# A gated hybrid decoder layer on one core: the first rows of x in one transfer, the gates' weights and a small load later, the gates' products in the second tile

## Chip, cores, metric

One NeuronCore of a Trainium2 chip. The metric is the device time of one execution in microseconds. TensorE is called PE, VectorE DVE, ScalarE ACT, GpSimd POOL, and SyncE, which only issues DMAs here, SP.

## What is computed

The layer has 512 rows of `x` with 2048 columns and multiplies them by one wide matrix; the columns of the result feed two kinds of attention, gates and a merge. Cut to what matters here:

```
h = x @ w_in                                  # (512 x 2048) @ (2048 x 11808)
log_f = log_sigmoid(h[fox_f] + b_f)           # 8 columns
gates = sigmoid(h[nsa_gate])                  # 24 columns
y_a = (fox_attention(..., log_f) * silu(h[fox_z])) @ w_a
y_b = (nsa_attention(..., gates, rel_bias) * silu(h[nsa_z])) @ w_b
out = layer_norm(ALPHA * x + (sigmoid(h[ga]) * y_a + sigmoid(h[gb]) * y_b) @ w_o)
```

The 8 + 24 columns of `log_f` and `gates` are called the gates' columns below.

## The kernel before

All products keep nearly full precision: each operand is split into a high part (`hi`, written by ACT) and a low part (`lo`, written by DVE; helper `split`, lines 96 and 97), and one product of float numbers becomes three matmuls (`mm3`, line 105). The gates' columns have a narrower form with two matmuls (`mm_two`, line 111).

A **tile** of the projection is 128 columns of `h`, computed as `h` transposed: 128 x 512 in one PSUM bank, summed over 16 blocks `k` of 128 rows of `w_in`, 48 matmuls. Its weights come in two **chunks** of 512 KB (tile `wr`, three buffers), each split in two **units** of four blocks `k`. `stream` walks through all units in order; ahead of unit n it splits the weights up to unit n + 3. After every second block `k` the helper `tick` takes one step of each background job in the list `active`, so what a job issues stands in each engine's queue between the matmuls. Each engine works through its own queue in order.

The first tile (columns `C_FZ`) is special, since `x` isn't on the chip yet. `load_x` loads `x`, in pieces of 128 rows by 256 or 512 columns; `transpose_x` transposes four 128 x 128 blocks on PE for each `k` (line 1462), splits the result into `big` (the resident transposed `x`), and lets ACT write one more copy (line 1466). `by_the_way` puts these steps ahead of the blocks k = 2, 4, 8 and 12 of the first tile, and with them the gates' products `gate_cols`: 8 matmuls ahead of k = 8 (with the split of the gates' weights `fgr` into `fgw`), 16 ahead of k = 12, 8 behind the tile. SP's queue, in order: `x` blocks 0 and 1 (four transfers), half of chunk 0, `x` 2 and 3, the other half, `x` 4 to 7, the gates' weights `fgr` (two transfers, 32 and 96 bytes a piece), chunk 1, `x` 8 to 15, chunk 2.

POOL issues small loads ahead of everything: the table `rel_bias` into `rb` and the bias `b_f` into `bf` (line 620), which reads the same 32 bytes for each of 128 partitions and four row blocks. Behind the first tile two jobs start: `lefts` (it waits ten ticks and then subtracts parts of `x` on DVE, line 1071, for later products) and `tables` (bias tables; products on PE at lines 637 and 644). The gates' job in `evac_fg` starts at the same point: transposes at line 681, then some 20 small operations on DVE with a step on ACT twice, then transposes at line 719 of what line 713 wrote, and a scan.

The buffers of tag `om` (16) hold `fgr`, the pieces of `x` and the jobs' small tiles; tag `a` (9) holds eight copies of `x` and the tile `zo` in which a finished tile leaves.

Of the kernel before, what the change touches and what calls it, by code (L numbers as in the profile page):

```python
# [12 lines left out]
F32 = mybir.dt.float32  # L13
# [7 lines left out]
P = 128  # L21
S = 512
D = 2048
KT = D // P
NT = S // P
H = 8
G = 2
HPG = 4
DH = 128
IN_COLS = 11808  # L30
C_FQ, C_FK, C_FV, C_FF, C_FZ = 0, 1024, 2048, 3072, 3080
C_NQ, C_KC, C_VC, C_KS, C_VS, C_KW, C_VW = 4104, 5128, 5384, 5640, 5896, 6152, 6408
C_NG, C_NZ, C_GA, C_GB = 6664, 6688, 7712, 9760
CMP_LEN, CMP_STRIDE, CMP_HID = 32, 16, 256
NCMP = (S - CMP_LEN) // CMP_STRIDE + 1
CP = 32
# [27 lines left out]
def layer(ctx, tc, x, w_in, b_f, pos_k, pos_v, wk1, wk2, wv1, wv2, w_a, w_b, w_o, ln_g, ln_b, rel, onehot, out):  # L64
    nc = tc.nc

    def dram(t, off, ap):
        return bass.AP(tensor=t.tensor, offset=t.offset + off, ap=ap)
# [21 lines left out]
    def bank(tag, bufs):  # L90
        return ps.tile([P, S], F32, name=tag, tag=tag, bufs=bufs)

    def split(hi, lo, src, scale=None):

        if scale is None:
            nc.scalar.activation(hi, src, AF.Copy)  # L96
            nc.vector.tensor_tensor(lo, src, hi.bitcast(F32), op=ALU.subtract)  # L97
        else:
            nc.scalar.activation(hi, src, AF.Copy, scale=scale)
            nc.vector.scalar_tensor_tensor(lo, src, scale, hi.bitcast(F32), op0=ALU.mult, op1=ALU.subtract)  # L100
# [140 lines left out]
    def proj(col, evac, **kw):  # L241
        dense(w_in, IN_COLS, col, D, x_src, evac, **kw)
# [12 lines left out]
    def pool(name):  # L255
        return stage[name][1]
# [42 lines left out]
    def evac_z_out(h):  # L299

        def f(p):
            t = out_tile()[:, 0]
            nc.scalar.activation(t, p, AF.Tanh, scale=0.5)
            nc.vector.scalar_tensor_tensor(t, t, 1.0, p, op0=ALU.add, op1=ALU.mult)
            nc.sync.dma_start(zd[h], t)
        return f
# [295 lines left out]
    def small(name, p, n):  # L602

        return pool("hd").tile([P, S], F32, name=name, tag="om", bufs=KT)[:p, :n]
# [11 lines left out]
    vd = dp.tile([S, H * DH], F32, name="v_d")  # L616
    sigd = [dp.tile([S, D], F32, name=f"sig_d{g}") for g in range(2)]

    nc.gpsimd.dma_start(rb, rel)
    nc.gpsimd.dma_start(bf, dram(b_f, 0, [[0, P], [0, NT], [1, H]]))  # L620

    def tables():
        po = small("po", 2 * CMP_LEN, DH)
        nc.gpsimd.dma_start(po[:CMP_LEN], pos_k[0])
        nc.gpsimd.dma_start(po[CMP_LEN:], pos_v[0])
        neg = small("neg", H, S)
        nc.vector.memset(neg, NEG)
        nc.gpsimd.dma_start(rel_d[:, S:2 * S], neg)
        nc.gpsimd.dma_start(rel_d[:, 2 * S:RL + S - 1], neg[:, :RL - S - 1])
        ohs = [small("oh", BUCKETS, S) for _ in range(2)]  # L630
        for c, oh in enumerate(ohs):
            nc.gpsimd.dma_start(oh, onehot[:, c * S:(c + 1) * S])
        for _ in range(4):
            yield
        for oh, at in zip(ohs, (0, RL + S - 1)):
            m = bank("m", 1)
            nc.tensor.matmul(m[:H], rb, oh, start=True, stop=True)
            tb = small("tb", H, S)
            nc.scalar.activation(tb, m[:H], AF.Copy)
            nc.gpsimd.dma_start(rel_d[:, at:at + S], tb)  # L640
            yield
        copies.append(spread())
        m = bank("m", 1)
        nc.tensor.transpose(m[:, :2 * CMP_LEN], po, ident[:2 * CMP_LEN, :2 * CMP_LEN])
        nc.vector.tensor_copy(posT, m[:, :2 * CMP_LEN])
        yield
# [24 lines left out]
    def evac_fg(p):  # L671

        fg = small("fg", 2 * CP, S)
        nc.vector.tensor_copy(fg, p[:2 * CP])

        def job():
            yield
            yield
            m = bank("m", 1)
            for i in range(NT):  # L680
                nc.tensor.transpose(m[:, i * 2 * CP:(i + 1) * 2 * CP], fg[:, i * P:(i + 1) * P], ident[:2 * CP, :2 * CP])
            mv = m[:, :NT * 2 * CP].rearrange("p (i u c) -> p i u c", u=2, c=CP)
            nc.vector.tensor_copy(gates, mv[:, :, 0, H:])
            nc.vector.tensor_tensor(gates, gates, mv[:, :, 1, H:], op=ALU.add)
            v, e, s, s2, acc = (small(n, P, NT * H).rearrange("p (i h) -> p i h", i=NT)
                                for n in ("fv", "fe", "fs", "fs2", "facc"))
            nc.vector.tensor_copy(v, mv[:, :, 0, :H])
            nc.vector.tensor_tensor(v, v, mv[:, :, 1, :H], op=ALU.add)
            nc.scalar.activation(gates, gates, AF.Tanh, scale=0.5)
            yield  # L690
            nc.vector.tensor_scalar(gates, gates, 1.0, 0.5, op0=ALU.add, op1=ALU.mult)

            nc.gpsimd.affine_select(gates[:, 0, 0::3], gates[:, 0, 0::3], pattern=[[0, H]], compare_op=ALU.is_ge,
                                    fill=0.0, base=-(CMP_LEN - 1), channel_multiplier=1)

            nc.vector.tensor_tensor(v, v, bf, op=ALU.add)
            nc.vector.tensor_scalar(s, v, -1.0, None, op0=ALU.mult)
            nc.vector.tensor_tensor(s, s, v, op=ALU.min)
            nc.scalar.activation(e, s, AF.Exp)
            yield  # L700
            nc.vector.tensor_scalar(s, e, 2.0, None, op0=ALU.add)
            nc.vector.reciprocal(s, s)
            nc.vector.tensor_tensor(s, s, e, op=ALU.mult)
            nc.vector.tensor_tensor(s2, s, s, op=ALU.mult)
            yield
            nc.vector.tensor_scalar(acc, s2, 1.0 / 17, None, op0=ALU.mult)
            for d in range(15, 2, -2):
                nc.vector.scalar_tensor_tensor(acc, acc, 1.0 / d, s2, op0=ALU.add, op1=ALU.mult)
            yield
            nc.vector.scalar_tensor_tensor(acc, acc, 1.0, s, op0=ALU.add, op1=ALU.mult)  # L710
            nc.vector.tensor_scalar(v, v, 0.0, None, op0=ALU.min)
            yield
            nc.vector.scalar_tensor_tensor(acc, acc, 2.0, v, op0=ALU.mult, op1=ALU.subtract)
            one, sums = small("fone", H, S), small("fsum", H, S)
            nc.gpsimd.memset(one, 1.0)
            yield
            m = bank("m", 1)
            for i in range(NT):
                nc.tensor.transpose(m[:H, i * P:(i + 1) * P], acc[:, i], ident)
            nc.vector.tensor_tensor_scan(sums, one, m[:H], 0.0, op0=ALU.mult, op1=ALU.add)  # L720
            nc.gpsimd.dma_start(negc_t, sums)
        active.append(job())
# [402 lines left out]
        ops.update({"B11": b_op(0, 0), "B21": b_op(1, 0), "B22": b_op(1, 1)})  # L1125
        pairs(jobs, ops, KT // 2, pairs_open)

    proj(C_FZ + DH, evac_z_out(1))
    for kv, c in (("k", C_KC), ("v", C_VC)):
        for g in range(G):  # L1130
            proj(c + g * DH, evac_raw(kv, g))
# [38 lines left out]
    sig, osp, fin = {}, {}, {}  # L1170
# [274 lines left out]
    fgr = small("fgr", P, S)  # L1445
    fgw = pool("hd").tile([P, KT, 2, CP], F32R, name="fgw")

    def load_x(*kts):

        c0, n = kts[0] * P, len(kts) * P  # L1450
        for i in range(NT):
            t = small("xn", P, n)
            nc.sync.dma_start(t, dram(x, i * P * D + c0, [[D, P], [1, n]]))
            for j, k in enumerate(kts):
                xn[k, i] = t[:, j * P:(j + 1) * P]

    def transpose_x(*kts):
        banks = []
# [9 lines left out]
    def gate_cols(*kts):  # L1468
        for k in kts:
            hi, lo = x_src(k)  # L1470
            mm_two(fin["fg"], CP, fgw[:, k].rearrange("p u c -> p (u c)"), hi, lo, k == 0, k == KT - 1)

    def by_the_way(k):
        if k == 0:
            fin["fg"] = bank("o", 1)
        elif k == 2:
            transpose_x(2, 3)
            split_w(1)
        elif k == 4:
            transpose_x(4, 5, 6, 7)  # L1480
            split_w(2)
        elif k == 8:
            transpose_x(*range(k, k + 4))
            split_w(3)
            split(fgw[:, :, 0], fgw[:, :, 1], fgr.rearrange("p (k c) -> p k c", c=CP))
            gate_cols(*range(4))
        elif k == 12:
            transpose_x(*range(k, k + 4))
            split_w(5)
            gate_cols(*range(4, 12))  # L1490

    def first_evac(p):
        gate_cols(*range(KT - 4, KT))
        evac_fg(fin["fg"])
        evac_z_out(0)(p)
        active.append(lefts())
        active.append(tables())

    rest = units[:]
    del units[:]  # L1500
    proj(C_FZ, first_evac, each=by_the_way)
    units += rest

    number_chunks()
    load_x(0, 1)
    load(0, between=lambda: load_x(2, 3))
    load_x(4, 5, 6, 7)
    for k0, (cc, cw) in ((0, (C_FF, H)), (H, (C_NG, 3 * H))):
        nc.sync.dma_start(fgr.rearrange("p (k c) -> p k c", c=CP)[:, :, k0:k0 + cw],
                          dram(w_in, cc, [[IN_COLS, P], [P * IN_COLS, KT], [1, cw]]))  # L1510
    load(1)
    load_x(8, 9, 10, 11)
    load_x(12, 13, 14, 15)
    load(2)
    split_w(0)
    transpose_x(0, 1)
    stream()
# [34 lines left out]
```

## Time and profile before

| | us |
|---|---|
| median of three runs | 1534.94 (1534.33 to 1535.65) |
| the profiled execution | 1535.65 |
| span of the profiled execution, first to last instruction | 1533.9 |
| PE busy | 1506.6 (98%) |
| DVE busy | 837.1 (55%) |
| ACT busy | 647.0 (42%) |

The profile belongs to the slowest of the three runs shown; 1.75 us of its time lie outside the span. Busy time of PE counts matmuls whose ends are modelled and overlap, so 98% says that PE is seldom without work, not that it works at its full clock.

### The profile page before, as it was taken

To read this page: it belongs to the slowest core of one execution; us is meant where nothing else is said; L and a number is where in the kernel's file an instruction comes from. 1 tells how busy PE (TensorE), PEld (TensorE's weight loads), DVE (VectorE), ACT (ScalarE), POOL (GpSimd) and SP (SyncE) were. 2 spreads that over 40 slices of the span, in tenths; PEclk is the share of its full clock that TensorE was granted. 3 is DMA by queue.
4 is the path that set the end of the run, shared out by engine and by line. 5 is a ranking of instruction groups with operands and counts; after the bars stand their busy time and mean duration, and the time that the engine had idled before them with its cause. 6 is when DMAs were issued, how large, how long until landed. Compare 5 with 4: busy or idle time off the path is not lost.

```text
span 1533.9 us, 19748 instructions
## 1 busy us (share of the span) xinstructions
PE 1506.6 (98%) x7161; PEld 1257.7 (82%) x7161; DVE 837.1 (55%) x1680; ACT 647.0 (42%) x1270; POOL 211.2 (14%) x351
## 2 busy tenths in 40 slices
PE   6999999999999999999999999999999999999998
PEld 4788787987898878888788888888888888888886
DVE  2666675666664664564445666356644443444455
ACT  4345556565554553443333444244444222222233
POOL 0201010211114541433000000000002010030001
PEclk9999999999999999999999999999999999999999
DMA  7568776877675452453233222332236343273236
GB/s 186 142 198 205 194 185 176 170 219 175 178 171 178 147 152 84 131 151 110 70 96 96 70 76 76 83 90 63 68 83 220 123 132 130 97 243 98 98 110 165
DMA packets 203009, 208.59 MB, mean 136 GB/s; under 512 B 12848, under 2 KB 153184, under 8 KB 202912
## 3 DMA queue, kind: packets, MB, share of 16 engines
q1 hardware_dynamic: 182016, 158.88, 34.8%
q0 software_dynamic: 20608, 47.93, 13.7%
q8 instruction: 56, 0.92, 0.2%
q10 hardware_dynamic: 288, 0.52, 0.1%
q14 instruction: 41, 0.34, 0.1%
HBM read 190.72 MB, written 20.22 MB: 138 GB/s over the span
## 4 chain that ended last, share of the span: by engine, by line
PE 93%; DVE 3%; ACT 2%; DMA 2%; issue 1%; POOL 0%; SPq 0%; ACTq 0%; DVEq 0%; POOLq 0%
PE d L105 51%; PE s L105 13%; PE pt L105 9%; PE o L105 9%; PE m L105 6%; DVE wl L97 2%; PE pt L417 2%; ACT wh L96 1%; DMA wr<-in_w_in_dram 1%; PE m L111 1%; PE o L111 1%; PE d L1236 0%; DMA sig_d<-zo 0%; DMA vT<-v_d 0%; PE pt L573 0%
## 5 line engine op out<-in xcount | busy, mean ns | idle before, releaser
L105 PE MATMUL d<-big,wh 128*128 128x512 f32 x1792 | 569.1, 398 | 6.2 <-ACT big L96 5.2
L97 DVE TENSOR_TENSOR wl<-wr,wh 128x512 fp32r<-128x512 f32 (+1 forms) x492 | 331.2, 681 | 378.6 <-ACT wh L96 368.2
L96 ACT ACTIVATE wh<-wr 128x512 fp32r<-128x512 f32 (+1 forms) x492 | 299.9, 618 | 393.1 <-PE d L105 136.7
L105 PEld LDWEIGHTS d<-big,wh 128*128 128x128 f32 x1792 | 324.9, 189 | 69.9 <-ACT big L96 5.9
L105 PE MATMUL d<-big,wl 128*128 128x512 f32 x896 | 351.7, 393 | 0.1
L105 PEld LDWEIGHTS d<-big,wl 128*128 128x128 f32 x896 | 168.8, 188 | 37.7 <-DVE wl L97 0.5
L399 ACT ACTIVATE p<-p,mn 128x128 f32<-128x128 f32 (+3 forms) x96 | 54.0, 562 | 133.6 <-DVE mn L397 133.6
L97 DVE TENSOR_TENSOR wl<-s,wh 128x512 fp32r<-128x512 f32 (+1 forms) x120 | 75.3, 637 | 54.5 <-ACT wh L96 54.1
L96 ACT ACTIVATE wh<-s 128x512 fp32r<-128x512 f32 (+1 forms) x120 | 69.0, 587 | 58.7 <-DVE wl L97 32.8
L105 PE MATMUL s<-wh,T 128*128 128x512 f32 (+1 forms) x320 | 93.2, 367 | 0.0
L105 PE MATMUL o<-wh,big 128*128 128x512 f32 (+1 forms) x224 | 84.3, 376 | 2.7 <-ACT wh L96 2.7
L105 PE MATMUL m<-wh,big 128*128 128x512 f32 (+1 forms) x224 | 83.7, 374 | 0.0
L105 PE MATMUL d<-wh,big 128*128 128x512 f32 (+1 forms) x240 | 74.4, 376 | 0.0
L97 DVE TENSOR_TENSOR pT<-pt,pT 128x512 fp32r<-128x512 f32 (+1 forms) x96 | 46.6, 488 | 44.6 <-ACT pT L96 44.2
L806 POOL TENSOR_SCALAR af<-raw,posT 128x31 f32<-128x31 f32 x128 | 66.1, 539 | 0.1
L105 PEld LDWEIGHTS s<-wh,T 128*128 128x128 f32 x320 | 59.2, 188 | 7.5
L96 ACT ACTIVATE pT<-pt 128x512 fp32r<-128x512 f32 (+1 forms) x96 | 41.1, 432 | 47.0 <-PE pt L417 46.3
L105 PE MATMUL s<-wl,T 128*128 128x512 f32 (+1 forms) x160 | 58.7, 367 | 0.0
L105 PEld LDWEIGHTS o<-wh,big 128*128 128x128 f32 x224 | 42.0, 188 | 10.6 <-ACT wh L96 4.6
L968 POOL DMA_DIRECT2D r<-in_w_in_dram x20 | 23.7, 1187 | 195.6 <-DVE wl L97 113.2
L105 PEld LDWEIGHTS d<-wh,big 128*128 128x128 f32 x240 | 44.7, 188 | 7.2 <-ACT wh L96 0.4
L489 POOL DMA_DIRECT2D bt<-skew_d x8 | 4.3, 541 | 324.9 <-DVE mn L397 257.5
(310 smaller groups left out, 2401.8 us busy)
## 6 DMA issues: line engine op xcount, KB each, us to landing
wr<-in_w_in_dram SPq DMA_DIRECT2D x147, 512.0 KB, 3.7
wr<-in_w_o_dram SPq DMA_DIRECT2D x32, 512.0 KB, 3.6
wr<-in_w_in_dram SPq DMA_DIRECT2D x24, 384.0 KB, 3.9
wr<-in_w_a_dram SPq DMA_DIRECT2D x16, 512.0 KB, 3.6
om<-sig_d POOLq DMA_DIRECT2D x32, 256.0 KB, 4.9
wr<-in_w_b_dram SPq DMA_DIRECT2D x16, 512.0 KB, 3.6
r<-in_w_in_dram SPq DMA_DIRECT2D x12, 512.0 KB, 4.9
r<-in_w_in_dram POOLq DMA_DIRECT2D x12, 512.0 KB, 10.8
```

What stands on the lines that cost most here:

```text
L96: nc.scalar.activation(hi, src, AF.Copy)
L97: nc.vector.tensor_tensor(lo, src, hi.bitcast(F32), op=ALU.subtract)
L105: nc.tensor.matmul(o, u, v, start=first and n == 0, stop=last and n == 2, **kw)
L111: nc.tensor.matmul(*u, start=first and u is whole, stop=last and u is whole)
L399: nc.scalar.activation(row, row, AF.Exp, bias=it["mn"][:, i:i + 1], scale=-1.0, accum_out=it["l"][:, i:i + 1])
L417: nc.tensor.transpose(b[:, (i - j) * P:(i - j + 1) * P], pt[:, OFF[i] + j * P:OFF[i] + (j + 1) * P], ident)
L489: nc.gpsimd.dma_start(bt, dram(skew_d, h * P * RL + P - 1, [[RL - 1, P], [1, S]]))
L806: nc.gpsimd.tensor_scalar(af[:, l, g], src, posT[:, po0 + ll:po0 + ll + 1], None, op0=ALU.add)
L968: nc.gpsimd.dma_start(two(n, k), rows(jobs[j], quad[0] * kh + k - 1, quad[1]), accum_op=ALU.add)
```

## The change

`x` blocks 0 and 1 come in one transfer of 512 KB instead of four, into a buffer of tag `a`, and blocks 2 and 3 in two instead of four. The gates' weights `fgr` go behind all of `x` and behind chunk 2 in SP's queue. The gates' products leave the first tile: their weights are split ahead of k = 4 of the second tile, 16 matmuls stand ahead of its k = 8 and 16 behind it, and the gates' job starts there, while `lefts` and `tables` still start behind the first tile. The second tile is therefore now set up beside the first, ahead of the others. The loads of `rb` and `bf` move into the job `tables`, `bf` behind the `onehot` tables.

```
--- before.py
+++ after.py
@@ -616,10 +616,8 @@
     vd = dp.tile([S, H * DH], F32, name="v_d")
     sigd = [dp.tile([S, D], F32, name=f"sig_d{g}") for g in range(2)]
 
-    nc.gpsimd.dma_start(rb, rel)
-    nc.gpsimd.dma_start(bf, dram(b_f, 0, [[0, P], [0, NT], [1, H]]))
-
     def tables():
+        nc.gpsimd.dma_start(rb, rel)
         po = small("po", 2 * CMP_LEN, DH)
         nc.gpsimd.dma_start(po[:CMP_LEN], pos_k[0])
         nc.gpsimd.dma_start(po[CMP_LEN:], pos_v[0])
@@ -630,6 +628,7 @@
         ohs = [small("oh", BUCKETS, S) for _ in range(2)]
         for c, oh in enumerate(ohs):
             nc.gpsimd.dma_start(oh, onehot[:, c * S:(c + 1) * S])
+        nc.gpsimd.dma_start(bf, dram(b_f, 0, [[0, P], [0, NT], [1, H]]))
         for _ in range(4):
             yield
         for oh, at in zip(ohs, (0, RL + S - 1)):
@@ -1125,7 +1124,6 @@
         ops.update({"B11": b_op(0, 0), "B21": b_op(1, 0), "B22": b_op(1, 1)})
         pairs(jobs, ops, KT // 2, pairs_open)
 
-    proj(C_FZ + DH, evac_z_out(1))
     for kv, c in (("k", C_KC), ("v", C_VC)):
         for g in range(G):
             proj(c + g * DH, evac_raw(kv, g))
@@ -1445,14 +1443,19 @@
     fgr = small("fgr", P, S)
     fgw = pool("hd").tile([P, KT, 2, CP], F32R, name="fgw")
 
-    def load_x(*kts):
+    def load_x(*kts, rows=1):
 
         c0, n = kts[0] * P, len(kts) * P
-        for i in range(NT):
-            t = small("xn", P, n)
-            nc.sync.dma_start(t, dram(x, i * P * D + c0, [[D, P], [1, n]]))
-            for j, k in enumerate(kts):
-                xn[k, i] = t[:, j * P:(j + 1) * P]
+        for i in range(0, NT, rows):
+            if rows == NT:
+                t = pool("tw").tile([P, rows * n], F32, name="xa", tag="a", bufs=KT // 2 + 1)
+            else:
+                t = small("xn", P, rows * n)
+            t = t.rearrange("p (i c) -> p i c", i=rows)
+            nc.sync.dma_start(t, dram(x, i * P * D + c0, [[D, P], [P * D, rows], [1, n]]))
+            for r in range(rows):
+                for j, k in enumerate(kts):
+                    xn[k, i + r] = t[:, r, j * P:(j + 1) * P]
 
     def transpose_x(*kts):
         banks = []
@@ -1471,9 +1474,7 @@
             mm_two(fin["fg"], CP, fgw[:, k].rearrange("p u c -> p (u c)"), hi, lo, k == 0, k == KT - 1)
 
     def by_the_way(k):
-        if k == 0:
-            fin["fg"] = bank("o", 1)
-        elif k == 2:
+        if k == 2:
             transpose_x(2, 3)
             split_w(1)
         elif k == 4:
@@ -1482,36 +1483,45 @@
         elif k == 8:
             transpose_x(*range(k, k + 4))
             split_w(3)
-            split(fgw[:, :, 0], fgw[:, :, 1], fgr.rearrange("p (k c) -> p k c", c=CP))
-            gate_cols(*range(4))
         elif k == 12:
             transpose_x(*range(k, k + 4))
             split_w(5)
-            gate_cols(*range(4, 12))
+
+    def gates_by_the_way(k):
+        if k == 0:
+            fin["fg"] = bank("o", 1)
+        elif k == 4:
+            split(fgw[:, :, 0], fgw[:, :, 1], fgr.rearrange("p (k c) -> p k c", c=CP))
+        elif k == 8:
+            gate_cols(*range(8))
 
     def first_evac(p):
-        gate_cols(*range(KT - 4, KT))
-        evac_fg(fin["fg"])
         evac_z_out(0)(p)
         active.append(lefts())
         active.append(tables())
 
+    def second_evac(p):
+        gate_cols(*range(8, KT))
+        evac_fg(fin["fg"])
+        evac_z_out(1)(p)
+
     rest = units[:]
     del units[:]
     proj(C_FZ, first_evac, each=by_the_way)
+    proj(C_FZ + DH, second_evac, each=gates_by_the_way)
     units += rest
 
     number_chunks()
-    load_x(0, 1)
-    load(0, between=lambda: load_x(2, 3))
+    load_x(0, 1, rows=NT)
+    load(0, between=lambda: load_x(2, 3, rows=2))
     load_x(4, 5, 6, 7)
-    for k0, (cc, cw) in ((0, (C_FF, H)), (H, (C_NG, 3 * H))):
-        nc.sync.dma_start(fgr.rearrange("p (k c) -> p k c", c=CP)[:, :, k0:k0 + cw],
-                          dram(w_in, cc, [[IN_COLS, P], [P * IN_COLS, KT], [1, cw]]))
     load(1)
     load_x(8, 9, 10, 11)
     load_x(12, 13, 14, 15)
     load(2)
+    for k0, (cc, cw) in ((0, (C_FF, H)), (H, (C_NG, 3 * H))):
+        nc.sync.dma_start(fgr.rearrange("p (k c) -> p k c", c=CP)[:, :, k0:k0 + cw],
+                          dram(w_in, cc, [[IN_COLS, P], [P * IN_COLS, KT], [1, cw]]))
     split_w(0)
     transpose_x(0, 1)
     stream()
```

## Rows read from the trace of the kernel before

**Rows 1.** The page, its first lines: the span of the profiled execution and the busy time of TensorE (PE), with its share of the span.

```profile
span 1533.9 us, 19748 instructions
...
PE 1506.6 (98%) x7161; PEld 1257.7 (82%) x7161; DVE 837.1 (55%) x1680; ACT 647.0 (42%) x1270; POOL 211.2 (14%) x351
```

**Rows 2.** The list of waits of PE from 0 to 80 us: engine, tile and line that waited, what ended the wait, total us, times, longest.

```profile
PE d L105 <- ACT big L96: 5.2, 1, 5.2
PE o L111 <- DVE fgw L97: 4.6, 1, 4.6
PE s L1462 <- DMA xn<-in_x_dram: 4.1, 2, 3.3
```

**Rows 3.** The same list from 80 us to the end: its longest row.

```profile
PE o L105 <- ACT wh L96: 2.7, 5, 0.6
```

**Rows 4.** Busy time in stretches of the first 36 us. Columns: from:to and length in us, busy us and instructions of PE, PEld, DVE, ACT and POOL, the granted clock as the profile prints it, the busy share of the DMA engines, GB/s.

```profile
6.95:12.10 5.15, 0.00 (x0) 0.00 (x0) 0.45 (x1) 1.11 (x3) 0.00 (x0) 1.00 0.67 195
12.15:18.36 6.21, 6.16 (x17) 4.29 (x18) 2.57 (x5) 3.33 (x6) 1.02 (x2) 1.00 0.94 216
18.36:25.95 7.59, 7.57 (x49) 6.38 (x47) 4.73 (x9) 6.95 (x14) 0.00 (x0) 1.00 1.01 325
25.95:30.57 4.62, 0.00 (x0) 0.00 (x1) 3.12 (x6) 3.75 (x8) 0.00 (x0) 0.80 0.79 243
30.57:35.32 4.75, 4.75 (x11) 2.73 (x12) 0.00 (x0) 0.00 (x0) 0.00 (x0) 0.50 0.41 114
```

**Rows 5.** The chain that ended last, in order of time (start us, us, what).

```profile
2.65 8.32 DMA wr<-in_w_in_dram
...
15.50 0.85 PE s L1462 x4
...
19.50 0.44 PE s L1462 x4
...
24.18 0.45 PE s L1462 x4
...
30.57 3.67 PE o L111 x8
...
39.38 3.69 PE o L111 x16
```

**Rows 6.** DMA issues, each row from the answer for a narrow window around its issue: the first block of `x` (issued at 0.80 us), the first half chunk of weights (2.65 us), the bias `bf` (2.22 us), and a whole weight chunk issued alone (29.94 us). Columns: size, us from issue to landing.

```profile
xn<-in_x_dram SPq DMA_DIRECT2D x1, 128.0 KB, 2.4
...
wr<-in_w_in_dram SPq DMA_DIRECT2D x1, 256.0 KB, 8.3
...
bf<-in_b_f_dram POOLq DMA_DIRECT2D x1, 16.0 KB, 8.0
...
wr<-in_w_in_dram SPq DMA_DIRECT2D x1, 512.0 KB, 3.5
```

**Rows 7.** DMA traffic in three stretches, one after the other: 3.5 to 4 us, 4.5 to 5 us, and 5 to 7 us with the queue that POOL's transfers use (packets that began there, MB, their time as a share of 16 engines over the stretch; a packet that lasts beyond the stretch counts whole).

```profile
DMA packets 154, 0.13 MB, mean 251 GB/s; under 512 B 32, under 2 KB 154, under 8 KB 154
...
DMA packets 2, 0.00 MB, mean 4 GB/s; under 512 B 0, under 2 KB 2, under 8 KB 2
...
DMA packets 202, 0.13 MB, mean 65 GB/s; under 512 B 12, under 2 KB 202, under 8 KB 202
...
q0 software_dynamic: 19, 0.02, 110.3%
```

**Rows 8.** The timeline of POOL's queue (start us, us, engine, line, operation) and, last, SP's issue of the two gate weight loads.

```profile
1.53 0.70 POOL L619 DMA_DIRECT2D rb<-in_rel_bias_dram  x1 [0.17 <-issue]
2.22 0.83 POOL L620 DMA_DIRECT2D bf<-in_b_f_dram  x1
...
17.28 0.53 POOL L624 DMA_DIRECT2D po<-in_cmp_pos_k_dram  x1 [14.23 <-PE pt L1462]
...
51.01 0.52 POOL L628 DMA_DIRECT2D rel_d<-neg  x1 [32.70 <-DVE neg L627]
...
11.83 3.69 SPq L1509 DMA_DIRECT2D fgr<-in_w_in_dram  x2
```

**Rows 9.** The timeline of ACT and DVE around the end of the first tile.

```profile
38.11 0.60 ACT L96 ACTIVATE big<-s 128x512 fp32r<-128x512 f32 x1 [8.41 <-PE s L1462]
...
41.94 1.22 ACT L96 ACTIVATE wh<-wr 128x512 fp32r<-128x512 f32 x2
42.68 1.29 DVE L97 TENSOR_TENSOR wl<-wr,wh 128x512 fp32r<-128x512 f32 x2 [1.45 <-ACT wh L96]
```

**Rows 10.** The job behind the gates, on PE and DVE, and the first subtractions of the job `lefts`; the last two rows are DVE's busy time in two stretches of that job (length, busy us and instructions, clock, DMA share, GB/s).

```profile
51.71 0.46 PE L681 MATMUL m<-ident,fg 64*128 64x64 f32 x4
...
57.57 1.02 PE L637 MATMUL m<-oh,rb 32*8 32x512 f32 x2
...
60.70 0.18 DVE L713 SCALAR_TENSOR_TENSOR facc<-facc,fv 128x32 f32<-128x32 f32 x1
...
63.17 0.60 PE L719 MATMUL m<-ident,facc 128*8 128x128 f32 x4
...
66.29 1.29 DVE L1071 TENSOR_TENSOR x<-x 128x512 f32<-128x512 f32 x2
...
52.15:54.20 2.05, 1.49 (x8) 1.00 0.96 272
55.25:58.20 2.95, 2.48 (x13) 1.00 0.55 155
```

## The prediction

> **What bounds the kernel.** The page comes first: PE is busy for 1506.6 of 1533.9 us [rows 1]. What can be won is its idle time and any time at a low clock. The list of PE's waits says where the idle time is: three waits of 5.2, 4.6 and 4.1 us ahead of 80 us [rows 2], and behind 80 us no kind of wait over 2.7 us in total [rows 3]. So behind the first two tiles the kernel is one stream of matmuls; what the start gains or loses should pass unchanged to the end. The first 48 us decide.
>
> The stretches [rows 4] show the start. PE stands still from 6.95 to 12.10 us, works until 25.95, stands still again until 30.57, and runs at the low level afterwards (granted 0.50, 1.2 GHz). From 12.15 to 18.36 the column prints 1.00, but four transposes take 0.85 us at 15.50 and 0.44 us at 19.50 [rows 5]: I take the first stretch for the low level too.
>
> The chain names the causes. The first idle stretch is the half chunk of weights issued at 2.65 us, which lands 8.32 us later, at 10.97 [rows 5]; PE's first product follows 1.2 us behind it. The second ends with the split of the gates' weights, and the first eight gate products then take 3.67 us where sixteen take 3.69 later [rows 5].
>
> **Why the first weights are late.** A whole chunk of 512 KB issued alone lands in 3.5 us; this half of one took 8.3 [rows 6]. Traffic is 251 GB/s at 3.5 us, 4 GB/s between 4.5 and 5, 65 GB/s between 5 and 7 [rows 7]. `bf` was issued at 2.22 us [rows 8], needed 8.0 us for 16 KB [rows 6] and so landed at about 10.2, and in the stretch from 5 to 7 us the 19 packets of POOL's queue have 110% of 16 engines' time, 35 us, for 0.02 MB [rows 7]. I read this as `bf` holding up everything else until about 10 us.
>
> **The change, part by part.** PE's time, one term after the other:
>
> *1. First product, -5.75 us.* A block of 128 KB landed in 2.4 us [rows 6]; at 325 GB/s [rows 4] its bytes are 0.4 of that, so some 2.0 us are fixed. One transfer of 512 KB (0.524 MB, 1.6 us) issued at 0.80 lands at 4.4, the half chunk behind it (0.8 us) at 5.2. Merging makes the first transposes wait for all four row blocks, but the eight end at 4.4 + 2 x 0.85 = 6.1, when the split weights aren't ready either: with the 1.2 us from weights to product it starts at 6.4, not 12.15. Bounds: if `bf` isn't the cause the weights land where they did, 0; if it held each engine only for the 35 us / 16 = 2.2 us of its own packets, -2.2. I stay near the upper end because nothing moved at all from 4.5 to 5.
>
> Here the Trainium skill (DMA: Bandwidth & Descriptors, "Queues, rings and completion order") says otherwise: an engine takes packets from its queues in turn, so a slow packet should hold the other queue for its own length only. By that rule the 2.2 us would be the whole price; the almost empty 4.5 to 5 us disagree. It is a rival below.
>
> *2. First product to k = 8, 0.* This takes 25.95 - 12.15 = 13.8 us, of which 6.21 at the low level. I keep it: PE again starts from rest. If the clock rises earlier, it is shorter by up to 6.21 / 2 = 3.1; supply could lengthen it. At 325 GB/s, with flow from about 2 us, `x` 4 to 7 are on chip by 10.1 and 8 to 11 by 14.9; their transposes, started at some 19.1 and 23.8 before (one group of four ahead of the rows in [rows 5]), now come 5.75 earlier, at 13.4 and 18.0. Some 3 us to spare. All of `x` is there at about 18.1, needed at 23.
>
> *3. The wait ahead of the gates' products goes: -4.6.* The products of k = 8 need only `big` and weights split before the gates' [rows 4].
>
> *4. The low level behind that wait goes: -2.2.* Eleven matmuls took 4.75 us [rows 4]; at 3.69 / 16 = 0.23 each [rows 5] they take 2.5.
>
> *5. The 32 gate matmuls move, 0.* They cost 32 x 0.23 = 7.4 us in either tile. Their weights' split (one ACT, one DVE operation) is hidden in the second tile's first eight blocks.
>
> *6. Cover lost ahead of the second tile: +0.8.* ACT began the last four splits at 38.11, and the second tile's `wl` came at 42.68 + 0.69 = 43.37: 5.26 us [rows 9]. The sixteen gate matmuls lay over this. Without them PE has three groups of transposes (1.3 us) and the 12 + 2 products ahead of the first use of `wl` (3.2): 4.5 us. Bounds 0 and 1.5.
>
> *7. `fgr` behind chunk 2, 0.* SP is held 3.69 us by its issue [rows 8], and now chunk 3 stands behind it. `x` ends at 18.1, chunk 2 (0.524 MB) at 19.7, `fgr` at 23.5, chunk 3 at about 27 (3.5 us). It serves the third unit of the second tile, some 5.5 us behind that tile's start at about 28, so more than 6 us remain; every microsecond beyond that would be PE's.
>
> *8. `rb` and `bf`, 0 beyond term 1.* `rb` stays at the front of POOL's queue, since nothing ahead of it there waits. Pieces of `x` and `fgr` now take 15 of the 16 `om` buffers, so `po`, which waited 14.23 us for one, can follow at about 2 us; two ordinary loads of 16 KB. `bf` now stands behind the transfer that waited for the memset of `neg` [rows 8]; that memset is in the second tile, so `bf` should run from about 32 us. If it again stops all traffic for 6 us, the weight chunks it delays are those of the tiles behind, needed over 10 us later; without that cover it would cost up to 6. Its reader comes about 20 us later.
>
> *9. The gates' job meets `lefts`: +1.9.* `lefts` still counts from the first tile, the gates' job now from the second, so both fall in the third. From the transposes at 51.71 to those at 63.17, PE took 11.5 us, of which 2 x 0.95 + 0.2 us table products that stay in the second tile: 9.4 us after the change. In that time DVE must do the job's 8 and 12 operations and three more (some 1.5 + 2.5 + 0.5 us [rows 10]), two weight splits (1.2), and now six subtractions of 0.6 (1.29 for two [rows 10]): 9.3. Latency at the start (0.5) and two waits in order for ACT's steps (some 0.7 each) make 11.2. DVE would then finish line 713 some 1.8 us behind PE, which waits there in order with all later products behind it; before, 713 ended 2.3 us ahead (60.70 to 63.17). Bounds: 0, if DVE gets further ahead, and 3.6, all six subtractions.
>
> Sum: -5.75 - 4.6 - 2.2 + 0.8 + 1.9 = -9.9 us. From the profiled 1535.65 that is 1525.8; the median of the runs is 0.7 lower, and from 1534.94 it is **1525.0**.
>
> **Rivals.**
>
> *A. As above:* chance 0.55, with its own range 1523.3 to 1526.9 (-11.6 to -8.0).
>
> *B. No jam in the third tile, or an earlier rise of the clock:* terms 9 or 2 give about 2 us back, 1523 (terms 9 and all of 2: 1520). DVE's 55% [rows 1] speaks for it; against it that its queue is in order. Chance 0.18.
>
> *C. The front opens only partly:* the packets' own time, -2.2 instead of -5.75, gives 1528.5; nothing at the front, 1530.7. For it: that other traffic, not `bf`, might be slow so early. Against it: the gap at 4.5 us. Chance 0.2.
>
> *D. Not faster: the clock doesn't rise in the first tile.* The products and transposes from k = 4 on (36 x 0.23 + 12 x 0.44 = 13.6 us) would take twice as long, +13.6, less the 9.9: 1538.6. It decides from 9.9 us more at the low level, on top of the 6.2 that I keep. For it: the first tile's work is now cut by short waits for splits. Against it: PE worked 6.16 of 6.21 us before it rose, waits of some 0.3 us included, and 4.62 us of standing still preceded the fall. Chance 0.03; 0.04 are left for a result within 0.2%.
>
> The Trainium skill (TensorE: Matmul & The Clock Gate, "Part 1") states that the low clock is the default and that sustained activity releases it; the two low stretches behind idle time agree.
>
> **Numbers.** A measurement of this kernel tells 0.2%, 3.1 us, from no change. Faster by more: A, B and C, 0.93; same 0.04; slower 0.03. The range reaches down over most of B and up over C's bound, -13.4 to -5: 1521.5 to 1530.0.
>
> **What would show it.** PE's first product near 6.4 us and the half chunk landing in some 4 us (term 1); no wait of `o` for `fgw` and no second low stretch (3, 4); the first tile over near 27 to 28 us, a wait under 1 us at its end (6); `bf` issued behind the `oh` loads, its slow packets beside idle-tolerant weight loads (8); and PE waiting at line 719 for line 713 (9). Wrong would be: the first weights still late with `bf` gone from there, PE's third tile without that wait, or a clock at 0.50 past 14 us.

## The result and the profile after

The changed kernel takes 1524.16 us (median of four runs, 1523.79 to 1525.12) where the kernel before takes 1534.63 (four runs): the ratio is 0.9934, with a 95% interval from 0.9916 to 0.9951. The forecast was 1525.0 us, with a range from 1521.5 to 1530.0.

The page has the same PE work in a shorter span; PE's busy time fell by 2.6 us [rows 1], about what term 4 of the prediction gives for matmuls that no longer run at the low level:

```profile
span 1523.4 us, 19742 instructions
...
PE 1504.0 (99%) x7161; PEld 1256.0 (82%) x7161; DVE 836.7 (55%) x1680; ACT 647.0 (42%) x1270; POOL 210.6 (14%) x351
```

PE's waits from 0 to 80 us, in the form of [rows 2]. The wait of `d` for `big` and that of `o` for `fgw` are gone, that for the first rows of `x` is one of 4.5 us, and three new ones have come, the longest at line 718 (line 719 before):

```profile
PE s L1465 <- DMA xa<-in_x_dram: 4.5, 1, 4.5
PE m L718 <- DVE facc L712: 1.3, 1, 1.3
PE d L105 <- ACT wh L96: 0.4, 1, 0.4
PE d L105 <- DVE big L97: 0.2, 1, 0.2
```

The chain in order of time (start, us, what; answers to [rows 5]):

```profile
1.28 3.92 DMA wr<-in_w_in_dram
...
19.90 2.91 PE d L105 x12
...
27.87 6.01 PE d L105 x24
33.88 3.69 PE o L111 x16
...
53.59 0.39 PE m L680 x4
...
63.72 0.60 PE m L718 x4
```

The half chunk of weights lands 3.92 us after its issue, at 5.20, not at 10.97. The first tile is followed directly by 24 matmuls of the second, and sixteen gate products together take 3.69 us, the price at the high level. The timeline of PE puts the first product at 6.39 us:

```profile
6.39 1.63 PE L105 MATMUL d<-big,wh 128*128 128x512 f32 x2
```

The gain stands where the prediction looked for it. In the chain of either kernel, before and after, the matmuls of line 105 into `pt` (the phase behind the seventh tile) begin 10.35 us apart, of the 10.5 us by which the spans differ:

```profile
116.84 10.88 PE pt L105 x48
...
106.49 10.88 PE pt L105 x48
```

The stretches (columns as in [rows 4]) have no idle stretch and no granted clock under 1.00; four transposes of blocks 2 and 3, though, still take 0.87 us at 9.73 in the chain, so PE begins at the low level as before:

```profile
6.39:19.90 13.51, 13.24 (x66) 10.39 (x65) 7.28 (x13) 10.49 (x20) 0.00 (x0) 1.00 1.06 340
19.90:27.30 7.40, 7.40 (x41) 5.94 (x39) 5.02 (x9) 7.28 (x16) 0.00 (x0) 1.00 0.76 170
27.30:28.80 1.50, 1.09 (x4) 0.50 (x4) 0.95 (x2) 1.50 (x5) 0.00 (x0) 1.00 0.05 14
```

The bias `bf` now stands in POOL's timeline at 33.79 us (answers to [rows 8]). The traffic of the microsecond from 36 to 37 shows what it does there, as in [rows 7]:

```profile
33.79 0.80 POOL L631 DMA_DIRECT2D bf<-in_b_f_dram  x1
```

```profile
DMA packets 11, 0.01 MB, mean 12 GB/s; under 512 B 2, under 2 KB 10, under 8 KB 11
...
q0 software_dynamic: 11, 0.01, 186.1%
```

It is the same stop, behind cover: a chunk of weights issued beside it takes 7.7 us to land, and PE doesn't wait. The 186% counts packets whole that last beyond the microsecond.

### The profile page after: what moved, and what is told of

Its sections match the earlier page's. It is cut to its first block, busy times and chain, and to the rows that moved or that the text cites. A ratio compares the mean times of both kernels' runs of the same rounds, so it can differ in the third digit from the quotient of the medians.

```text
span 1523.4 us, 19742 instructions
## 1 busy us (share of the span) xinstructions
PE 1504.0 (99%) x7161; PEld 1256.0 (82%) x7161; DVE 836.7 (55%) x1680; ACT 647.0 (42%) x1270; POOL 210.6 (14%) x351
## 4 chain that ended last, share of the span: by engine, by line
PE 92%; DVE 4%; ACT 2%; DMA 1%; issue 1%; POOL 0%; SPq 0%; ACTq 0%; DVEq 0%; POOLq 0%
PE d L105 50%; PE s L105 13%; PE pt L105 9%; PE o L105 9%; PE m L105 6%; DVE wl L97 2%; PE pt L417 2%; ACT wh L96 1%; PE m L111 1%; PE o L111 0%; PE d L1234 0%; DMA sig_d<-zo 0%; DVE c L993 0%; DVE s L992 0%; DMA vT<-v_d 0%
```

## The experiments

Each ratio below is to runs of the kernel before in the same set and on the same chip. They took 1534.47 us in the set of the loads at the front (`bf` alone, `bf` back at the front, four transfers, the first run with other rows), 1534.25 in that of the jobs (the changed kernel again, the subtractions later, weights ahead of the copies, both edits) and 1534.50 in that of the last four runs (the gates' weights early, the second run with other rows, the shorter padding, two steps more). Differences to "the changed kernel" go by its 1524.16 us where the set of the jobs isn't named.

**The load of bf alone.** Edit, to the kernel before:

```
-    nc.gpsimd.dma_start(bf, dram(b_f, 0, [[0, P], [0, NT], [1, H]]))     # front of POOL's queue
+        nc.gpsimd.dma_start(bf, ...)                                     # in tables(), behind the onehot loads
```

> The kernel before, with the load of bf alone moved behind the onehot loads; all else stays where it was. If bf holds up all traffic until about 10 us: the first half chunk of weights, issued at 2.65 us as before, lands at about 5.7, the first product starts near 6.9 and the time falls by some 5.2 us to about 1529.5, with both the wait for the gates' weights (4.6 us) and the low clock behind it still there. If bf holds an engine only for its own packets (2.2 us): landing near 8.8, about 1532.5. If the slow start has another cause: first product at 12, time unchanged.

Measured 1538.08 us, ratio 1.0021 (1.0012 to 1.0031): slower. The chain:

```profile
2.65 3.46 DMA wr<-in_w_in_dram
...
27.15 3.63 PE o L111 x8
...
48.95 6.60 DMA bf<-in_b_f_dram
```

one row of SP's timeline and three of PE's:

```profile
7.55 5.40 SPq L1509 DMA_DIRECT2D fgr<-in_w_in_dram  x2
...
7.30 1.64 PE L105 MATMUL d<-big,wh 128*128 128x512 f32 x2 [1.15 <-ACT big L96]
...
47.62 0.46 PE L681 MATMUL m<-ident,fg 64*128 64x64 f32 x4
...
66.26 0.60 PE L719 MATMUL m<-ident,facc 128*8 128x128 f32 x4
```

one row of PE's waits from 10 to 30 us and two of all waits from 40 to 75 us:

```profile
PE s L1462 <- DMA xn<-in_x_dram: 0.9, 3, 0.3
...
DVE fv L696 <- DMA bf<-in_b_f_dram: 6.4, 1, 6.4
...
PE m L637 <- ACT tb L639: 4.0, 1, 4.0
```

and two stretches (columns as in [rows 4]), the second behind PE's wait at line 637:

```profile
53.40:57.59 4.19, 0.16 (x2) 0.00 (x1) 1.07 (x4) 1.23 (x3) 0.00 (x0) 1.00 0.00 0
57.59:62.00 4.41, 4.41 (x9) 1.93 (x9) 3.35 (x16) 1.11 (x2) 2.11 (x4) 0.53 0.45 128
```

The very front is as my theory had it: the weights land at 6.11 and the first product comes at 7.30 instead of 12.15, 4.85 us earlier. The first gate products come at 27.15 instead of 30.57 [rows 5], only 3.4 us earlier: on the way PE waits 0.9 us for later blocks of `x`, which SP issues from 14.20 us on, when the two `fgr` loads ahead of them have held it from 7.55 to 12.95. And line 719 comes at 66.26, 3.1 us later than before [rows 10]: the gates' job still starts behind the first tile, its DVE operation at line 696 waits 6.4 us for `bf`, ACT waits in order behind that and PE behind ACT, 4.0 us. Behind this wait PE is granted 0.53 until 64.88 us. From line 681 to line 719 it takes 18.6 us where it took 11.5 [rows 10]; the wait is 4.0 of the difference, and the other 3.1 go with the low level. So the expectation of the time failed: I had priced the new place of the load and not its reader, nor the low level behind a new wait. In the change the same load is harmless: `bf` is issued at 33.79, and the gates' products, and with them its reader, went one tile back.

**The load of bf back at the front.** Edit, to the changed kernel:

```
+    nc.gpsimd.dma_start(rb, rel)
+    nc.gpsimd.dma_start(bf, dram(b_f, 0, [[0, P], [0, NT], [1, H]]))
     def tables():
-        nc.gpsimd.dma_start(rb, rel)
...
-        nc.gpsimd.dma_start(bf, dram(b_f, 0, [[0, P], [0, NT], [1, H]]))
```

> The changed kernel with rb and bf back at the front of POOL's queue. If bf is the cause: the first half chunk lands again at 10 to 11 us, the first product near 11.5, and some 5 us are lost: about 1529.2. By the packets' own length: 2.2 us lost, 1526.4. If the single transfer lets the first weights through before bf's reads begin at about 4 us: under 1.5 us lost, 1525.5 or less, and the second blocks of x late instead.

Measured 1528.31 us (ratio 0.9965, 0.9954 to 0.9977; runs from 1527.43 to 1531.86), 4.2 us over the changed kernel. The chain shows which transfer is late, the second half of blocks 2 and 3; below it stands the same transfer in the changed kernel, from the DMA issues (256 KB, us to landing):

```profile
2.37 11.24 DMA xn<-in_x_dram
```

```profile
xn<-in_x_dram SPq DMA_DIRECT2D x1, 256.0 KB, 6.8
```

It lands at 13.6, while the first weights come through ahead of the stop: the first product is at 6.80 us. Two rows of PE's timeline, and one from that of the changed kernel:

```profile
13.66 0.69 PE L1466 MATMUL s<-ident,xn 128*128 128x128 f32 x2 [2.85 <-DMA xn<-in_x_dram]
...
18.06 1.05 PE L1466 MATMUL s<-ident,xn 128*128 128x128 f32 x4
```

```profile
13.33 0.60 PE L1465 MATMUL s<-ident,xn 128*128 128x128 f32 x4
```

The gates' products begin at 39.38 us in the chain, 5.5 later than in the changed kernel (33.88): 0.4 by the first product, 2.9 by the wait for `x`, and most of the rest because the low level lasts longer; the next transposes still take 1.05 us where they took 0.60. The amount is near the first theory's 5 us, the way is the third's, whose price of under 1.5 us left out the low level and held the wait too short. What `bf` no longer hits, since the single transfer lets the weights be issued at 1.28 us, is the first half chunk.

**Four transfers again.**

```
-            nc.sync.dma_start(t, dram(x, i * P * D + c0, [[D, P], [P * D, rows], [1, n]]))
+            for r in range(rows):        # where rows == NT
+                nc.sync.dma_start(t[:, r], dram(x, r * P * D + c0, [[D, P], [1, n]]))
```

> The changed kernel with blocks 0 and 1 of x in four transfers again, into the same tile. My theory gives the single transfer little: the half chunk of weights is issued 1.4 us later and lands about 0.5 us later (5.7), so the first product is at 6.9 and the time 1524.6. The rival, that the merging opened the start: first product at 9 or later, 1527 or more.

Measured 1526.71 us (0.9949, 0.9935 to 0.9964), 2.6 over the changed kernel. The half chunk is issued at 2.64 and lands at 6.97, and the first product comes at 8.16, 1.8 us later than in the changed kernel:

```profile
2.64 4.33 DMA wr<-in_w_in_dram
```

```profile
8.16 1.64 PE L105 MATMUL d<-big,wh 128*128 128x512 f32 x2 [1.58 <-ACT big L96]
```

I had 0.5 us for this and am wrong by 1.3: 1.4 us of later issue weigh in full, and the landing takes 0.4 longer. With four transfers and without early `po` loads (the run with `bf` alone) the same transfer landed after 3.46 us; whether those loads make the difference wasn't tried. The merging is worth some 2 us here, not nothing.

**Other rows in place of bf's.** An extra load of the same shape at the front, but with 512 different addresses:

```
+    nc.gpsimd.dma_start(rb, rel)
+    nc.gpsimd.dma_start(other, dram(x, 0, [[D, P], [2 * H, NT], [1, H]]))
```

It ran twice: with its tile taken behind the padding that aligns the large tiles, and with it ahead of the padding.

> The changed kernel with one more small load at the front of POOL's queue, of the same shape as bf (128 partitions, four pieces of 32 bytes each) but from 512 different places in x, into a tile that nothing reads. If the many small pieces make bf slow, this stops the traffic too: as with bf at the front, about 5 us lost, 1529. If it is that all 512 pieces read the same 32 bytes, nothing is lost beyond 0.5 us: 1524.2 to 1524.7.

> The load of 512 pieces from different places again, its tile now taken ahead of the padding, so that the large tiles behind it keep their addresses. If the 14 us of the first such run came from the shifted addresses and the load costs nothing: 1524.2 to 1525. If the load itself costs: 1529 or more.

> The changed kernel with the padding 128 bytes a partition shorter and nothing else: the tiles behind it, with the resident transposed x first, lie 128 bytes lower. If the addresses made the first such run slow: about 1538.5, spread over the whole run. If not: 1524.2.

The first took 1538.93 us (1.0027, 1.0016 to 1.0038), the second 1524.85 (0.9939, 0.9924 to 0.9954); the first product came at 6.50 and 6.45. So the load costs the start nothing that shows. The traffic from 6 to 8 us of the second run, beside that with `bf` at the front, where the stop begins near 6 us:

```profile
DMA packets 676, 0.48 MB, mean 239 GB/s; under 512 B 55, under 2 KB 653, under 8 KB 676
...
q0 software_dynamic: 61, 0.03, 21.0%
```

```profile
DMA packets 186, 0.15 MB, mean 74 GB/s; under 512 B 14, under 2 KB 178, under 8 KB 186
...
q0 software_dynamic: 21, 0.02, 146.2%
```

With one address 21 packets of POOL's queue take 146% of 16 engines' time, with many 61 take 21%. So it is not the number of small pieces that stops the traffic; what differs is that one place is read again and again. The two loads also read different tensors, which no run separates. The second isn't free for the other transfers: the changed kernel, without it, moves 311 GB/s in this stretch.

The 14 us of the first run are no matter of the load. They are spread over the groups of matmuls that read `big`; the rows of the longest group in the changed kernel and in that run, 5.7 us of it:

```profile
L105 PE MATMUL d<-big,wh 128*128 128x512 f32 x1792 | 568.7, 398 | 1.4 <-ACT wh L96 1.1 <-DVE big L97 0.2
```

```profile
L105 PE MATMUL d<-big,wh 128*128 128x512 f32 x1792 | 574.4, 401 | 0.7 <-ACT wh L96 0.4 <-ACT big L96 0.2
```

Shorter padding alone, though, costs nothing (1523.13 us, 0.9929, 0.9914 to 0.9943). The first run had both the shorter padding ahead of `big` and the new tile behind it, so the distance of `big` from what follows was another. That this distance is the cause is a guess; it stays open.

**The subtractions later.**

```
     def lefts():
-        for _ in range(10):
+        for _ in range(16):
```

> The changed kernel, unchanged, beside the next three on the same chip: about 1524.2 us, with a wait of 1.3 us at line 718 for line 712 and about 0.8 us lost ahead of the second tile.

> The changed kernel with the job of the subtractions waiting 16 ticks instead of 10, so that it starts when the gates' job is nearly through. If the two jobs' meeting on DVE makes PE wait: that wait of 1.3 us is gone or under 0.2, and the time 1.3 us lower, about 1522.9. Rival: the later job ends too late for the phase behind the seventh tile, and PE waits there as long: unchanged or slower.

The changed kernel itself took 1525.26 us in this set, this one 1528.35 (0.9964, 0.9951 to 0.9976). The wait at line 718 is gone, as the first theory said. The rival holds for the time, 3.1 us more: among its waits from 90 to 112 us, in the phase behind the seventh tile, is

```profile
PE pt L105 <- ACT wh L96: 2.8, 1, 2.8
```

and the chain passes for some 11 us ahead of that, from 97 to 108 us, through splits on ACT and DVE of the tile `T`. Put off, the job isn't ready in time and is waited for.

**Weights ahead of the copies.** In `transpose_x`, for k = 12:

```
+        if ahead is not None:
+            split_w(ahead)
         for k, b in zip(kts, banks):
             nc.scalar.activation(left["x"][k // 2][:, k % 2], b, AF.Copy)
```

> The changed kernel with the weights of the second tile's first unit split ahead of ACT's last four copies of x instead of behind them. If the lost cover is what PE waits for ahead of the second tile (0.4 us for wh, 0.43 for wl): both waits gone, 0.8 us lower, about 1523.4. Rival: the wait moves to the unit behind, whose weights still follow the copies: no more than 0.3 us lower.

Measured 1523.30 us (0.9929, 0.9916 to 0.9941), 2.0 less than the changed kernel beside it (1525.26). The wait for `wh` ahead of the second tile is gone from the list. In the profiled executions the gates' products begin at 32.48 us instead of 33.61, 1.1 earlier, of which 0.15 stood already at the transposes of block 4 (13.08 for 13.23); the 1.0 left is near the forecast 0.8. The rest of the 2.0 isn't explained by the edit; it lies within what such executions differ by behind the start (see the last section).

**Both edits.**

> Both of these: 1.3 + 0.8 = 2.1 us lower than the changed kernel, about 1522.1, if the two waits are separate. If one of them only moves, about 1523.

1527.23 us (0.9955, 0.9942 to 0.9969): 1.1 less than with the later subtractions alone, but 2.0 more than the changed kernel beside it. Both expected times failed, since they left out the late job's 2.8 us, which are there unchanged.

**The gates' weights early.** The two `fgr` loads back behind `load_x(4, 5, 6, 7)`:

> The changed kernel with the gates' weights back behind blocks 4 to 7 of x in SP's queue, their products still in the second tile. Chunk 1 and the eight later loads of x come some 3.7 us later. If the supply had the 3 us to spare that the prediction gave it: at most 1 us lost, up to 1525.2. If the opened start needs these transfers out of the way: 2 us or more, 1526.2 and above, with PE waiting for blocks 8 and up.

1525.70 us (0.9943, 0.9927 to 0.9960), 1.5 over the changed kernel's first set and 0.4 over its second, between the two expected ranges: inconclusive for the time. PE's list shows no wait for `x` behind the first blocks, so the way of the second theory did not occur; the gates' products begin 0.8 us later (34.50 for 33.72), in a run whose first four transposes of blocks 2 and 3 took 0.85 us, the low level.

**Two steps more for the gates' job,** with the weights first:

```
             yield
+            yield
+            yield
             m = bank("m", 1)
             for i in range(NT):
                 nc.tensor.transpose(m[:H, ...], acc[:, i], ident)
```

> The changed kernel with the weights split ahead of ACT's copies (as in the run that did that alone) and the gates' job waiting two ticks more ahead of its last transposes, so that PE comes to them 2.7 us later; the subtractions start where they did. If DVE only needs this time: the wait of 1.3 us at those transposes is gone and, other than with the later subtractions, nothing is late behind it: 2 to 3 us below the changed kernel, 1521.5 to 1522.5. If the jam is too long for that: a wait is left and 1523 or more.

Measured 1520.93 us (0.9916, 0.9901 to 0.9930), 3.2 us under the changed kernel and the fastest of all. Some of that is luck: in the profiled execution the transposes of blocks 4 and up begin 1.2 us earlier (12.13 for 13.33) by an earlier rise of the clock, which no edit here aims at. PE's waits from 0 to 130 us are those of the start and two splits:

```profile
PE s L1467 <- DMA xa<-in_x_dram: 4.3, 1, 4.3
PE d L105 <- ACT big L96: 0.3, 1, 0.3
PE d L105 <- DVE big L97: 0.2, 1, 0.2
```

So the jam of the two jobs is what PE waited for at line 718: taken away from either side the wait is gone. Moved from the gates' side, it leaves no new wait of PE up to 130 us.

## Why the prediction was right, step by step

*First product (forecast -5.75).* 6.39 us for 6.4, the landing at 5.20 for 5.2. The size was right, its make-up in part, and so the close match is partly luck: as the expectation of the run with four transfers says, I gave nearly all of it to `bf` and little to the single transfer. The runs say that each of the two edits without the other already lets the first weights land early (6.97 at the latest), and that with the single transfer alone `bf` hits the next one. Undoing the merging of blocks 0 and 1 costs 2.6 us, undoing `bf`'s move 4.2; they overlap. The upper bound that I chose, that the stop lasts until `bf` has landed and not only for its packets' own 2.2 us an engine, held: with `bf` at the front the second half of blocks 2 and 3 takes 11.24 us instead of 6.8, 4.4 longer, and lands at 13.6, 0.4 us behind `bf` (issued at 2.21, 11.0 us to landing).

The Trainium skill (DMA: Bandwidth & Descriptors, "Queues, rings and completion order") gives each queue its turn behind a packet. By that rule alone the transfer should be held for about one such packet, 2.2 us; the trace has 4.4 and decides.

*First product to k = 8 (0).* From 6.39 to 19.90, 13.5 us for 13.8 [rows 4]. PE did not wait for `x` in between.

*Gates' wait and low clock (-4.6, -2.2).* Both gone, as the list of waits and the stretches show. No run undoes the move of the gates' products alone. That these terms belong to it rests on the lists: the wait of `o` for `fgw` stands at 4.6 us before and with `bf` alone, and in no run with the products in the second tile.

*Ahead of the second tile (+0.8).* 0.4 us for `wh` in the list, and in 27.30 to 28.80 PE is busy for 1.09 of 1.50 us. The list has no wait for `wl`, but the first three products of the second tile take 1.06 us from start to start (27.87 to 28.93) and the next three 0.70. Together that is near the 0.8, and the run with the weights first gets about 1.0 us back there.

*`fgr` late (0).* No wait of the third unit or of the gates' products. The issue of `fgr` holds SP for 5.28 us, not the 3.69 of the forecast; chunk 3, issued at 20.69, still lands at 25.8, ahead of the forecast 27. The reverse run doesn't say more.

*`bf` late (0).* It stops the traffic again, at a place where 6 us are covered. That the cover of its reader was needed as well, the run with `bf` alone shows: 6.4 us on DVE, 4.0 on PE and the low level behind them, more than the whole gain.

*The jobs' meeting (+1.9).* PE waits 1.3 us at line 718, from transposes at 53.59 to 63.72, 10.1 us for the 11.2 I had given DVE, with six subtractions in between as forecast. The term was right in kind and 0.6 too large. I had given each of ACT's two steps 0.7 us of waiting, and DVE's list shows one wait of 0.82; PE without its wait took 8.8 us, not the 9.4 that I had, so the two errors partly cancel. (11.2 less 9.4 is 1.8; the sum took 1.9.)

With the terms as measured, -5.8 - 0.3 - 4.6 - 2.2 + 0.8 + 1.3 = -10.8; the spans differ by 10.5. Of the rivals, B's lack of a jam didn't occur. C's partial opening didn't either; that the run with `bf` at the front lands near its 1528.5 is a coincidence, since its first product is early. D didn't: the clock had risen before block 4, whose transposes take 0.60 us from 13.33, where those of blocks 2 and 3 took 1.05 from 9.53.

## What to carry to other kernels

In the first microseconds ask of each load what it makes wait, not how many bytes it has: 32 bytes read 512 times from one place, 16 KB in all, took the traffic of 16 DMA engines down for some 5 us. When a load or a product is moved, follow its reader too: the same move of `bf` cost 3.6 us alone, where PE lost 4.0 us to the wait and some 3.1 to the low clock behind it, and was free once its reader had moved some 20 us back. And where two background jobs come to overlap on an engine that works in order, look for the matmul behind the later one's last step; here a few steps of slack were free in the job that nobody waits for soon, and not in the job with an end to meet.

## What the runs showed of the hardware

A load that reads the same 32 bytes 512 times held the traffic down for microseconds. From 4.0 to 8.5 us the kernel before moves 55 GB/s and the changed kernel 272 (columns as in [rows 4]):

```profile
4.00:8.50 4.50, 2.08 (x7) 1.11 (x6) 0.00 (x0) 0.00 (x0) 0.00 (x0) 1.00 0.68 55
```

```profile
4.00:8.50 4.50, 4.00 (x12) 2.93 (x13) 1.89 (x3) 2.91 (x5) 0.00 (x0) 1.00 0.96 272
```

The same shape over 512 addresses did not (239 GB/s from 6 to 8 us, where `bf` leaves 74). SP's own issues slow down with it: four loads of `x` hold SP for 5.29 us in the kernel before and for 1.93 with `bf` moved, from the same time on:

```profile
3.12 5.29 SPq L1453 DMA_DIRECT2D xn<-in_x_dram  x4
```

```profile
3.12 1.93 SPq L1453 DMA_DIRECT2D xn<-in_x_dram  x4
```

How one address does this stays open. It isn't only that the long packets occupy the engines: in the kernel before, the traffic is at 4 GB/s between 4.5 and 5 us [rows 7], when no packet of POOL's queue begins. A transfer issued ahead of it gets through almost untouched, first product at 6.80 us for 6.39, and one issued 1.1 us later takes 11.24.

The moment of the clock's rise differs between runs with the same start. In the changed kernel four transposes begun at 9.73 us still took 0.87 us, in the run with the shorter padding four begun at 9.02 took 0.45 (both in the chain), with the first product at 6.39 and 6.35:

```profile
9.73 0.87 PE s L1465 x4
```

```profile
9.02 0.45 PE s L1465 x4
```

The gates' products then begin at 33.72 and 32.55 us. So about 1 us between executions with this start need be no effect of an edit, unless the trace shows the wait that went. The Trainium skill (TensorE: Matmul & The Clock Gate, "Part 1") says that the moment varies between runs; these two rows agree.

The long part behind the start varies by more. From the first matmul into `pt` behind the seventh tile to the end, which no edit touches, the shorter padding takes 1415.5 us (1520.9 - 105.36) and the second run with other rows 1418.2 (1524.5 - 106.34), at equal matmul times (398 ns in the longest group of either):

```profile
105.36 10.88 PE pt L105 x48
```

```profile
106.34 10.88 PE pt L106 x48
```

What makes the difference isn't settled. A gain of 1 or 2 us at the start is better read from the times at the start than from the whole time.

With a tile of 128 bytes a partition at another place, the matmuls that read `big` were about 1% slower (398 to 401 ns in the longest group as the profile gives them); the whole kernel took 14 us more. Why stays open.
